# Two groups of vector work moved in the merging stage of a fused decoder block: the sums of a weight pair, and the split of one weight unit behind the third gate

## The chip, the cores and the metric

The kernel runs on one core of a Trainium2 chip. A core has a matrix engine (PE, with its weight loads shown apart as PEld), a vector engine (DVE), a scalar engine (ACT), a small general engine (POOL), and an engine that mostly issues transfers (SP, whose queue is called SPq). They run side by side; each takes its own instructions strictly in the order in which the program lists them, and they wait for each other through semaphores. The metric is the time of one execution in microseconds, as the median of several runs.

## The reference, cut to what matters

The program computes one decoder layer for 256 positions of 1024 features in float32: a SwiGLU feed-forward part, a mixing part with two branches, a second feed-forward part and a final norm. The change lies in the mixing part:

```python
n = rmsnorm(h, mix_norm[l])
z = n @ w_in[l]
q, k, v = z[..., :512], z[..., 512:1024], z[..., 1024:1536]
attn = moba_attention(to_heads(q), to_heads(k), to_heads(v))        # causal, 8 heads
zg = gelu(z[..., 1536:])
gm = chunked_spatial_gating(zg[..., :512], zg[..., 512:], ...)      # u * (W_s layernorm(v) + b)
y_attn = attn @ w_branch_attn[l]
y_gmlp = gm @ w_branch_gmlp[l]
gates = sigmoid(n @ w_gate[l] + b_gate[l])                          # 256 x 2048
merged = gates[..., :1024] * y_attn + gates[..., 1024:] * y_gmlp
h = h + merged @ w_out[l]
```

With 256 positions and blocks of 256 keys, the attention is plain causal attention.

## The kernel before, in words

**Precision.** Every float32 product is made from three matmuls: both operands are split into a high part (a rounded copy, made by ACT) and a low part (the rest, made by DVE as source minus high). The helper `split` at L259 records this pair: ACT's `CAST w<-raw` at L260, then DVE's `TENSOR_TENSOR w<-raw,w` at L262. All weights of the layer pass through it once, so most of ACT's and DVE's work is the splitting of weights.

**Weights.** A weight arrives as a unit of two halves. Each half is one load of 512 KB by SP into a buffer called `raw`, of which there are seven in a ring (L182); its split goes to a buffer `w`, of which there are five in a ring (L167). A load can go into its `raw` buffer only when DVE has made the low part of the half that lay there seven halves earlier. `split_half` (L185) records the split of the next half, after asking for the loads that the ring allows; with `later=True` the ACT part is recorded at once and the DVE part when the caller calls back. `unit(i, ahead)` (L221) records all splits up to unit i + ahead that haven't been recorded yet, so a call of it with nothing left to do records nothing.

**Pairs.** For some weights a scheme with seven products instead of eight is used. It needs sums and differences of the weights: the unit with the word "sums" is made from two loaded halves by four additions on DVE (L209 to L212, 128 x 512 each), and then split like a loaded one (`CAST w<-sum`, `TENSOR_TENSOR w<-sum,w`). For the columns u (of the spatial gating) and v (of the attention), there are two such pairs; the change concerns the sums of the second.

**Order of work.** PE, SP and, in the mixing part, also ACT and DVE take their instructions in the order in which the Python code records them (`in_order`, and the schedule in `kernel`). There is no planner there: to move a line in the code moves its instructions on the engine's queue.

**The mixing part in the order of time.**

- The chunks q, k and gv (the input of the layer norm in the spatial gating) are multiplied. q and k are scaled by ACT and transposed by DVE (`turn_qk`, L845: ACT L848, DVE L849), written to DRAM and read back in another layout (`qback`, and kT inside the tile `qk`; the read back is `from_way`, L566).
- gv goes through a gelu on ACT (L979) and `layer_norm` on DVE (from L951 on). The pair product `accuv` gives u and v (DVE L432 to L446). Then come the scores `sc` of the attention (PE L863; their evacuation is ACT L869 and DVE L870), the spatial mix `mix`, the exponents (ACT L880) and the probabilities with their transposes (DVE L890, L893), which go to DRAM and come back by keys.
- The four gate chunks `g` (512 columns each) are multiplied. For each, `gate` (L926) records first the ACT half of some splits of later weights, if it is asked for them, then two DVE evacuations (L931) and two sigmoids on ACT (L933), then the DVE half of those splits.
- In between, the gating's output is transposed, written to DRAM and read back as `gmback`; `settle_in` (L575) splits it into the tile `gm` (`gmT` in the code).
- `attend` (L937) gives `po`, split into the tile `ao`. `merge` (L1037) multiplies `gm` with the branch weights bg (`pg`) and `ao` with the branch weights ba (`pa`), first for columns 0 to 511, then for 512 to 1023; DVE gates both (L1043, L1054), adds them (L1055) and transposes them (L1056) into `mt`, which goes to DRAM (`mway`) and comes back split as `mg`.
- The output projection follows (`down_features`, `acc`, L229 and L234), in four units of two blocks of `mg` each, and then the second feed-forward part, which takes the rest of the time.

The units after the gates are, in this order, bg0, ba0, bg1, ba1 (two halves each), then four units `out`.

Of the kernel before, what the change touches and what calls it, by code (L numbers as in the profile page):

```python
# [10 lines left out]
F32 = mybir.dt.float32  # L11
# [7 lines left out]
P = 128  # L19
# [34 lines left out]
def block_kernel(ctx, tc, t, out):  # L54
    nc = tc.nc
# [3 lines left out]
    sump = ctx.enter_context(tc.tile_pool(name="sump", bufs=2))  # L59
# [7 lines left out]
    def bank(name):  # L67
        return psum.tile([P, 512], F32, tag="ps", name=name)
# [42 lines left out]
    def add_units(name, n):  # L111
        first = len(units)
        units.extend((name, i) for i in range(n))
        return first
# [25 lines left out]
    muv = len(units)  # L140
    units.extend(("uvs", i, what) for i in range(PAIR_UV) for what in ("single", "sums"))
    units.extend([("u", 0), ("v", 0)])
    mg = add_units("gate", 8)
# [12 lines left out]
    def kind(i):  # L156
        return units[i][2] if len(units[i]) > 2 else None

    parts, raws = {}, {}
# [25 lines left out]
    def split_half(later=False):  # L185

        i, hf = divmod(done_to[0], 2)
        if hf == 0:
            unit_tile(i)
        fetch_to(done_to[0] + RAW)  # L190
        done_to[0] += 1
        if kind(i):
            return quarters(i, hf)
        w, sl = parts[i], half(i, hf)
        return split(w[:, sl, 0, :], w[:, sl, 1, :], raws.pop((i, hf)), later)

    def quarters(i, hf):

        w = parts[i]
        if kind(i) == "single":  # L200
            r = raws[i, hf].rearrange("p one (n c) -> p (one n) c", c=512)
            r, to = (r, w[:, 1:3]) if hf else (r[:, :1], w[:, :1])
        else:
            if hf == 0:
                (a, b), (c, d) = ([r[:, 0, n:n + 512] for n in (0, 512)] for r in [raws.pop((i - 1, k)) for k in range(2)])
                for k in range(2):
                    raws[i, k] = sump.tile([P, 2, 512], F32, tag="sum", name=f"sum{i}_{k}")
                first, second = raws[i, 0], raws[i, 1]
                nc.vector.tensor_add(first[:, 0], a, b)  # L209
                nc.vector.tensor_add(first[:, 1], b, d)  # L210
                nc.vector.tensor_add(second[:, 0], first[:, 0], d)
                nc.vector.tensor_add(second[:, 1], second[:, 0], c)  # L212
            r, to = raws.pop((i, hf)), w[:, 2 * hf:2 * hf + 2]
        return split(to[:, :, 0, :], to[:, :, 1, :], r)

# [5 lines left out]
    def unit(i, ahead=PAIRED):  # L221
        split_to(i + 1 + ahead)
        return parts[i]
# [29 lines left out]
    def mm3(ps, st, mv_, first, last):  # L253
        (sh, sl), (mh, ml) = st, mv_
        nc.tensor.matmul(ps, sh, mh, start=first, stop=False)  # L255
        nc.tensor.matmul(ps, sh, ml, start=False, stop=False)  # L256
        nc.tensor.matmul(ps, sl, mh, start=False, stop=last)  # L257

    def split(hi, lo, src, later=False):  # L259
        nc.scalar.copy(hi, src)  # L260
        def rest():
            nc.vector.tensor_sub(lo, src, hi.bitcast(F32))  # L262
        return rest if later else rest()

    def alloc_T(name, tags):

        return [act.tile([P, 4, 2, S], F32R, tag=tag, name=f"{name}{c}") for c, tag in enumerate(tags)]
# [4 lines left out]
    def block_of(nT, k):  # L272
        return both_of(nT, k)[:, 0, :], both_of(nT, k)[:, 1, :]
# [278 lines left out]
    def chunk(i0, nT, name, c, us=range(2), ps=None, apart=1, ahead=ALONE):  # L552

        if ps is None:
            ps = [bank(f"{name}_{c}{j}") for j in range(NT)]
        for u in us:
            w = unit(i0 + 2 * c + apart * u, ahead)
            for k in range(4):  # L560
                for j in range(NT):
                    st = tuple(p[:, j * P:(j + 1) * P] for p in block_of(nT, 4 * u + k))
                    mm3(ps[j], st, (w[:, k, 0, :], w[:, k, 1, :]), u + k == 0, u == 1 and k == 3)
        return ps
# [7 lines left out]
    def by_token(way):  # L572
        return way.rearrange("(j p) a n -> p j (a n)", p=P)

    def settle_in(to, back):  # L575

        to = to.rearrange("p k two (q c) -> p two q k c", c=32)
        split(to[:, 0], to[:, 1], back.rearrange("p q (k c) -> p q k c", c=32))
# [86 lines left out]
    for k in range(KB):  # L665
# [3 lines left out]
        x, w, g = row[:, :S], row[:, S:], front[:, k:k + 1]  # L669
# [78 lines left out]
    nT2 = alloc_T("n2", ("nA", "nB"))  # L748
# [3 lines left out]
    with in_order():  # L752
# [30 lines left out]
        for n, (at, s) in enumerate(f1d):  # L783
# [6 lines left out]
            else:  # L790
# [3 lines left out]
                for slot, j in [(x, j) for j in range(NT) for x in slots] if ends else [(x, j) for x in slots for j in range(NT)]:  # L794
                    f, b = divmod(slot, len(REST))
# [33 lines left out]
        def tokens(blocks):  # L829
            return blocks.rearrange("p (j a) t -> p j (a t)", j=NT)  # L830
# [14 lines left out]
        def turn_qk(i, ps):  # L845
            by_tokens = tokens(mix_a[:, 8 + 4 * i:12 + 4 * i])
            for j in range(NT):
                nc.scalar.activation(by_tokens[:, j], ps[j], AF.Copy, scale=rs2[j])  # L848
                nc.vector.transpose(qk_turned[i][:, j], by_tokens[:, j])  # L849
# [76 lines left out]
        def gate(g, ps, splits=0):  # L926

            c = slice(g * 512, (g + 1) * 512)
            lows = [split_half(True) for _ in range(2 * splits)]
            for j in reversed(range(NT)):  # L930
                nc.vector.scalar_tensor_tensor(gates[:, j, c], ps[j], rs2[j], gates[:, 0, c],  # L931
                                               op0=ALU.mult, op1=ALU.add)
                nc.scalar.activation(gates[:, j, c], gates[:, j, c], AF.Sigmoid)  # L933
            for low in lows:
                low()
# [29 lines left out]
        turn_qk(0, psq)  # L965
        chunk(mk, nT2, "k", 0, [1], psk, 3, DEEP)
        nc.sync.dma_start(by_token(qk_way[0]), qk_turned[0])
        turn_qk(1, psk)
        nc.sync.dma_start(by_token(qk_way[1]), qk_turned[1])
        q_back = tmp.tile([P, S // 32, P], F32, tag="back", name="qback", bufs=1)  # L970
# [44 lines left out]
        gm_back = tmp.tile([P, S // 32, P], F32, tag="back", name="gmback", bufs=1)  # L1015
        from_way(gm_back, gm_way)
        gate(1, chunk(mg, nT2, "g", 1, [1], psg), 1)
        gate(2, chunk(mg, nT2, "g", 2), 1)
        settle_in(gmT, gm_back)
        gate(3, chunk(mg, nT2, "g", 3))  # L1020

# [221 lines left out]
```

## Time and profile before

| | |
|---|---|
| median of 3 runs | 516.3 us (516.11 to 516.36) |
| profiled execution, its own time | 516.4 us |
| span of its instructions | 514.7 us |
| PE busy | 505.0 us (98%) |
| DVE busy | 462.1 us (90%) |
| ACT busy | 309.9 us (60%) |
| mean granted PE clock | 0.993 |

The profiled execution took 1.7 us more than the span from its first to its last instruction. Times in the profile count from the span's start. "Idle before" in square brackets behind a row is the time in which the engine stood still before that instruction, with what ended it. A row with "x4" merges four instructions in a row; its time is that of the group. Busy times of PE overlap a little, since matmuls are pipelined.

### The profile page before, as it was taken

How to read it: one execution, taken by the hardware profiler on the slowest of the kernel's cores; microseconds unless marked ns; L12 is line 12 of the kernel's file. 1: busy time of each engine (PE TensorE's matmuls, PEld its weight loads, DVE VectorE, ACT ScalarE, POOL GpSimd, SP SyncE). 2: the span in 40 equal slices, each digit the busy share in tenths (PEclk: the TensorE clock that was granted, in tenths of full speed). 3: DMA queues.
4: the chain of work that ended last, by engine and by line, in shares of the span. 5: the costliest groups of instructions: out<-in, count | busy, mean ns of one | idle time of the engine just before them, and what ended most of it. 6: DMA issues, size and time to landing. Idle time of an engine off the chain costs nothing.

```text
span 514.7 us, 6830 instructions
## 1 busy us (share of the span) xinstructions
PE 505.0 (98%) x2314; PEld 418.7 (81%) x2314; DVE 462.1 (90%) x675; ACT 309.9 (60%) x444; POOL 11.2 (2%) x25
## 2 busy tenths in 40 slices
PE   9999999999999999999999999999999999999995
PEld 6888888888888888888888877888888888888884
DVE  6898999999997989799894876998989989999995
ACT  7985549646564766765952803768635756565533
POOL 0010000000000010000000000001000000000001
PEclk9999999999999999999999998999999999999998
DMA  8998588798765987786789765937789648998402
GB/s 317 375 330 327 156 276 258 267 307 280 228 220 179 308 282 291 184 291 245 232 218 304 287 202 171 295 120 260 257 274 300 213 140 274 350 327 251 177 1 82
DMA packets 63987, 126.82 MB, mean 246 GB/s; under 512 B 11729, under 2 KB 36817, under 8 KB 63825
## 3 DMA queue, kind: packets, MB, share of 16 engines
q1 hardware_dynamic: 63664, 126.06, 74.4%
q8 instruction: 18, 0.29, 0.3%
q10 hardware_dynamic: 288, 0.33, 0.2%
q14 instruction: 17, 0.13, 0.1%
HBM read 113.26 MB, written 13.11 MB: 246 GB/s over the span
## 4 chain that ended last, share of the span: by engine, by line
PE 94%; DVE 2%; DMA 2%; issue 1%; ACT 1%; SPq 0%; POOLq 0%; DVEq 0%; POOL 0%; ACTq 0%
PE f L255 12%; PE f L257 12%; PE f L256 12%; PE accdown L257 4%; PE accdown L255 4%; PE accdown L256 4%; PE acch L257 3%; PE acch L255 3%; PE acch L256 3%; PE acc L229 3%; PE g L255 3%; PE g L256 3%; PE g L257 3%; PE acc L234 1%; PE accuv L256 1%; PE accuv L257 1%
## 5 line engine op out<-in xcount | busy, mean ns | idle before, releaser
L262 DVE TENSOR_TENSOR w<-raw,w 128x1024 fp32r<-128x1024 f32 (+1 forms) x180 | 202.7, 1163 | 18.0 <-ACT w L260 17.6
L260 ACT CAST w<-raw 128x1024 fp32r<-128x1024 f32 (+1 forms) x180 | 173.2, 1007 | 31.4 <-DMA raw<-in_ba 8.3
L257 PE MATMUL f<-w,n 128*128 128x512 f32 x272 | 105.8, 389 | 0.0
L255 PE MATMUL f<-w,n 128*128 128x512 f32 x272 | 105.8, 389 | 0.0
L256 PE MATMUL f<-w,n 128*128 128x512 f32 x272 | 105.8, 389 | 0.0
L257 PEld LDWEIGHTS f<-w,n 128*128 128x128 f32 x272 | 51.1, 188 | 10.7
L256 PEld LDWEIGHTS f<-w,n 128*128 128x128 f32 x272 | 51.1, 188 | 10.6
L255 PEld LDWEIGHTS f<-w,n 128*128 128x128 f32 x272 | 51.1, 188 | 10.5
L260 ACT CAST w<-sum 128x1024 fp32r<-128x1024 f32 x34 | 35.8, 1052 | 37.6 <-DVE sum L210 29.5
L262 DVE TENSOR_TENSOR w<-sum,w 128x1024 fp32r<-128x1024 f32 x34 | 41.0, 1216 | 0.5 <-ACT w L260 0.5
L256 PE MATMUL accdown<-w,f1h 128*128 128x512 f32 x68 | 26.5, 389 | 0.0
L257 PE MATMUL accdown<-w,f1h 128*128 128x512 f32 x68 | 26.5, 389 | 0.0
L255 PE MATMUL accdown<-w,f1h 128*128 128x512 f32 x68 | 26.5, 389 | 0.0
L255 PE MATMUL g<-w,n 128*128 128x512 f32 x64 | 25.0, 391 | 0.0
L257 PE MATMUL g<-w,n 128*128 128x512 f32 x64 | 24.9, 389 | 0.0
L256 PE MATMUL g<-w,n 128*128 128x512 f32 x64 | 24.9, 389 | 0.0
L256 PE MATMUL acch<-w,f2h 128*128 128x512 f32 x59 | 23.0, 389 | 0.0
L257 PE MATMUL acch<-w,f2h 128*128 128x512 f32 x59 | 23.0, 389 | 0.0
L255 PE MATMUL acch<-w,f2h 128*128 128x512 f32 x59 | 23.0, 389 | 0.0
L229 PE MATMUL acc<-mg,w 128*128 128x512 f32 x64 | 18.7, 420 | 2.2 <-DVE mg L262 2.2
L596 ACT ACTIVATE f2s<-f,rstd 128x256 f32<-128x256 f32 x18 | 8.2, 474 | 14.0 <-PE f L257 13.9
L229 PEld LDWEIGHTS acc<-mg,w 128*128 128x128 f32 x64 | 12.2, 205 | 4.2 <-DVE mg L262 2.4
(291 smaller groups left out, 917.0 us busy)
## 6 DMA issues: line engine op xcount, KB each, us to landing
raw<-in_f SPq DMA_DIRECT2D x72, 512.0 KB, 6.5
raw<-in_f2d SPq DMA_DIRECT2D x22, 512.0 KB, 6.8
raw<-in_gate SPq DMA_DIRECT2D x16, 512.0 KB, 5.9
raw<-in_f1s SPq DMA_DIRECT2D x14, 512.0 KB, 6.4
raw<-in_f1d SPq DMA_DIRECT2D x14, 512.0 KB, 5.0
raw<-in_out SPq DMA_DIRECT2D x8, 512.0 KB, 5.3
raw<-in_f2s SPq DMA_DIRECT2D x6, 512.0 KB, 6.7
f1way<-f1t SPq DMA_DIRECT2D x11, 256.0 KB, 6.3
```

The lines of the kernel that those rows point to most:

```text
L229: nc.tensor.matmul(ps, st, both.rearrange("p two n -> p (two n)"), start=first, stop=last)
L234: nc.tensor.matmul(ps[:, n:], st, both[:, 0, :], start=False, stop=False)
L255: nc.tensor.matmul(ps, sh, mh, start=first, stop=False)
L256: nc.tensor.matmul(ps, sh, ml, start=False, stop=False)
L257: nc.tensor.matmul(ps, sl, mh, start=False, stop=last)
L260: nc.scalar.copy(hi, src)
L262: nc.vector.tensor_sub(lo, src, hi.bitcast(F32))
L596: nc.scalar.activation(sg, ps[j][:, :CH], AF.Silu, scale=rs[j])
```

## The change

Two places are changed.

**The third gate.** `gate(2, ...)` no longer records splits. Before, it put the ACT half of the split of unit ba0 (two halves) ahead of its own evacuation and sigmoids, and the DVE half behind them; `settle_in(gmT, gm_back)` was recorded after that. Now the third gate's evacuation and sigmoids come first, then the split of the gating's input `gm`, and the split of ba0 is recorded after it, when the fourth gate's chunk asks for its weights.

**The second pair's sums.** The four additions move into a function of their own, `quarter_sums`, which is called right after the second half of the chunk k and the issue of q's write to DRAM, ahead of `turn_qk(1, psk)`. When the split of that unit is recorded later, the sums are found made.

```diff
+    def quarter_sums(i):
+        (a, b), (c, d) = ([r[:, 0, n:n + 512] for n in (0, 512)] for r in [raws.pop((i - 1, k)) for k in range(2)])
+        for k in range(2):
+            raws[i, k] = sump.tile([P, 2, 512], F32, tag="sum", name=f"sum{i}_{k}")
+        first, second = raws[i, 0], raws[i, 1]
+        nc.vector.tensor_add(first[:, 0], a, b)
+        nc.vector.tensor_add(first[:, 1], b, d)
+        nc.vector.tensor_add(second[:, 0], first[:, 0], d)
+        nc.vector.tensor_add(second[:, 1], second[:, 0], c)
+
     def quarters(i, hf):
...
-            if hf == 0:
-                (a, b), (c, d) = ([r[:, 0, n:n + 512] for n in (0, 512)] for r in [raws.pop((i - 1, k)) for k in range(2)])
...
-                nc.vector.tensor_add(first[:, 0], a, b)
-                nc.vector.tensor_add(first[:, 1], b, d)
-                nc.vector.tensor_add(second[:, 0], first[:, 0], d)
-                nc.vector.tensor_add(second[:, 1], second[:, 0], c)
+            if hf == 0 and (i, 0) not in raws:
+                quarter_sums(i)
             r, to = raws.pop((i, hf)), w[:, 2 * hf:2 * hf + 2]
...
         chunk(mk, nT2, "k", 0, [1], psk, 3, DEEP)
         nc.sync.dma_start(by_token(qk_way[0]), qk_turned[0])
+        quarter_sums(muv + 3)
         turn_qk(1, psk)
...
         gate(1, chunk(mg, nT2, "g", 1, [1], psg), 1)
-        gate(2, chunk(mg, nT2, "g", 2), 1)
+        gate(2, chunk(mg, nT2, "g", 2))
         settle_in(gmT, gm_back)
         gate(3, chunk(mg, nT2, "g", 3))
```

No instruction is added or removed on any engine, and the order on PE, SP and POOL stays as it was. ACT's queue differs at one place, DVE's at two.

On ACT, at the third gate, it stood so before; `w_2515` is ba0, `w_2556` is bg1, and `mixed` holds the gates here:

```order
L260 CAST w_2482<-raw_1_2366 128x2x512
L260 CAST w_2515<-raw_0_2377 128x2x512
L260 CAST w_2515<-raw_1_2413 128x2x512
L933 ACTIVATE mixed<-mixed 128x512 x2
L260 CAST gm_1866<-gmback 128x8x4x32
L260 CAST w_2556<-raw_0_2417 128x2x512
L260 CAST w_2556<-raw_1_2445 128x2x512
L933 ACTIVATE mixed<-mixed 128x512 x2
```

and now (ba0 is `w_2523` here; line numbers behind the new function are three or four higher):

```order
L263 CAST w_2482<-raw_1_2366 128x2x512
L936 ACTIVATE mixed<-mixed 128x512 x2
L263 CAST gm_1866<-gmback 128x8x4x32
L263 CAST w_2523<-raw_0_2377 128x2x512
L263 CAST w_2523<-raw_1_2413 128x2x512
L263 CAST w_2556<-raw_0_2417 128x2x512
L263 CAST w_2556<-raw_1_2445 128x2x512
L936 ACTIVATE mixed<-mixed 128x512 x2
```

The two casts of ba0 went behind the two sigmoids and the cast of `gm`. On DVE the same place reads before:

```order
L931 SCALAR_TENSOR_TENSOR mixed<-g_2454,rstd_1769,mixed 128x512
L262 TENSOR_TENSOR w_2515<-raw_0_2377,w_2515 128x2x512
L262 TENSOR_TENSOR w_2515<-raw_1_2413,w_2515 128x2x512
L262 TENSOR_TENSOR gm_1866<-gmback,gm_1866 128x8x4x32
L262 TENSOR_TENSOR w_2556<-raw_0_2417,w_2556 128x2x512
```

and now:

```order
L934 SCALAR_TENSOR_TENSOR mixed<-g_2454,rstd_1769,mixed 128x512
L265 TENSOR_TENSOR gm_1866<-gmback,gm_1866 128x8x4x32
L265 TENSOR_TENSOR w_2523<-raw_0_2377,w_2523 128x2x512
L265 TENSOR_TENSOR w_2523<-raw_1_2413,w_2523 128x2x512
L265 TENSOR_TENSOR w_2556<-raw_0_2417,w_2556 128x2x512
```

The low part of `gm` went ahead of the two of ba0. On DVE at the turning of k (the transposes of `mixed` here are k's) it stood so before:

```order
L262 TENSOR_TENSOR w_1924<-raw_1_1820,w_1924 128x2x512
L849 STREAM_TRANSPOSE mixed<-mixed 128x512 x2
L209 TENSOR_TENSOR sum_0_1974<-raw_0_1780 128x512
L210 TENSOR_TENSOR sum_0_1974<-raw_0_1780,raw_1_1820 128x512
L211 TENSOR_TENSOR sum_1_1975<-sum_0_1974,raw_1_1820 128x512
L212 TENSOR_TENSOR sum_1_1975<-sum_1_1975,raw_1_1820 128x512
L262 TENSOR_TENSOR w_1973<-sum_0_1974,w_1973 128x2x512
```

and now:

```order
L265 TENSOR_TENSOR w_1924<-raw_1_1820,w_1924 128x2x512
L202 TENSOR_TENSOR sum_0_1956<-raw_0_1780 128x512
L203 TENSOR_TENSOR sum_0_1956<-raw_0_1780,raw_1_1820 128x512
L204 TENSOR_TENSOR sum_1_1957<-sum_0_1956,raw_1_1820 128x512
L205 TENSOR_TENSOR sum_1_1957<-sum_1_1957,raw_1_1820 128x512
L852 STREAM_TRANSPOSE mixed<-mixed 128x512 x2
L265 TENSOR_TENSOR w_1979<-sum_0_1956,w_1979 128x2x512
```

The four sums went ahead of k's two transposes; the casts of the sums on ACT stayed behind ACT's scaling of k.

More of the change, by code (lines that the diff above doesn't have):

```diff
@@ L203, in quarters @@
         else:
-            if hf == 0:
-                (a, b), (c, d) = ([r[:, 0, n:n + 512] for n in (0, 512)] for r in [raws.pop((i - 1, k)) for k in range(2)])
[L206 to L209, printed above, removed]
-                nc.vector.tensor_add(first[:, 1], b, d)
-                nc.vector.tensor_add(second[:, 0], first[:, 0], d)
-                nc.vector.tensor_add(second[:, 1], second[:, 0], c)
+            if hf == 0 and (i, 0) not in raws:
+                quarter_sums(i)
             r, to = raws.pop((i, hf)), w[:, 2 * hf:2 * hf + 2]
```

## The prediction

> **What bounds the kernel now.** I read the waits of PE first, then its granted clock around the one wait that counts, then the chain of waits back from there.
>
> ```profile
> PE acc L229 <- DVE mg L262: 2.2, 1, 2.2
> 309.00:310.00 1.00, 0.02 (x1) 0.03 (x1) 0.50 (x2) 0.71 (x2) 0.00 (x0) 0.84 0.57 130
> 310.00:311.00 1.00, 1.00 (x3) 0.81 (x4) 0.86 (x2) 0.00 (x0) 0.00 (x0) 0.50 0.62 175
> 313.00:314.00 1.00, 1.00 (x8) 0.87 (x8) 0.97 (x2) 0.69 (x1) 0.00 (x0) 0.95 0.69 279
> ```
>
> In the waits, the columns are total, times and longest. Past the warm-up PE stands still once: 2.2 us, before the output projection. In the stretches the clock is the third number from the right: 0.84 from 309, 0.50 from 310, 0.95 from 313. The pause thus costs a second time, in matmuls at half speed. Everything else is PE at work, so a gain must come from this place, and a loss from a new pause.
>
> ```profile
> 309.98 3.54 PE L229 MATMUL acc<-mg,w 128*128 128x512 f32 x8 [2.20 <-DVE mg L262]
> 313.35 1.12 PE L234 MATMUL acc<-mg,w 128*128 128x256 f32 x8
> 322.68 3.84 PE L229 MATMUL acc<-mg,w 128*128 128x512 f32 x16
> 326.35 2.08 PE L234 MATMUL acc<-mg,w 128*128 128x256 f32 x16
> 321.42 0.76 DVE L262 TENSOR_TENSOR mg<-mixed,mg 128x256 fp32r<-128x256 f32 x2 [2.34 <-ACT mg L260]
> ```
>
> PE is done with merging at 309.98 - 2.20 = 307.78 and starts the projection at 309.98. Its first eight matmuls take 313.35 - 309.98 = 3.37 us; sixteen later ones take 326.35 - 322.68 = 3.67, so eight at full clock 1.84. The slow clock costs 3.37 - 1.84 = 1.53 us. The last row is the next thing due: the third unit of the projection (PE, 322.68) needs the third piece of `mg`, whose first half is there at 321.42 + 0.76/2 + some 0.05 = 321.85. That leaves 0.8 us of slack.
>
> The chain back from the pause:
>
> ```profile
> 301.54 0.72 DVE mt L1056
> 306.67 2.29 DMA mixed<-mway
> 309.50 0.44 DVE mg L262
> ```
>
> The merged values leave DVE at 302.26 and need 7.2 us through DRAM and the split. Before that, from 288 on, DVE has no long break and waits only for ACT's casts, which themselves follow its evacuations: whatever it has done earlier brings PE's start forward one for one, until the pause is used up.
>
> **The third gate: removed wait, added wait.** ACT first, then DVE, then the landing of `gmback` (last column, from issue):
>
> ```profile
> 273.58 1.05 ACT L260 CAST w<-raw 128x1024 fp32r<-128x1024 f32 x1 [1.36 <-DMA raw<-in_ba]
> 281.56 1.05 ACT L260 CAST w<-raw 128x1024 fp32r<-128x1024 f32 x1 [6.93 <-DMA raw<-in_ba]
> 282.52 1.15 ACT L933 ACTIVATE mixed<-mixed 128x512 f32<-128x512 f32 x2
> 283.57 1.03 ACT L260 CAST gm<-gmback 128x1024 fp32r<-128x1024 f32 x1
> 284.51 2.00 ACT L260 CAST w<-raw 128x1024 fp32r<-128x1024 f32 x2
> 274.84 1.22 DVE L262 TENSOR_TENSOR w<-raw,w 128x1024 fp32r<-128x1024 f32 x1
> 282.65 1.22 DVE L262 TENSOR_TENSOR w<-raw,w 128x1024 fp32r<-128x1024 f32 x1 [6.59 <-ACT w L260]
> 284.63 1.22 DVE L262 TENSOR_TENSOR gm<-gmback,gm 128x1024 fp32r<-128x1024 f32 x1 [0.76 <-ACT gm L260]
> 285.77 2.35 DVE L262 TENSOR_TENSOR w<-raw,w 128x1024 fp32r<-128x1024 f32 x2
> 288.05 1.53 DVE L931 SCALAR_TENSOR_TENSOR mixed<-g,rstd,mixed 128x512 f32<-128x512 f32 x2
> 269.55 2.15 SPq L570 DMA_DIRECT2D gmback<-gmway  x4
> gmback<-gmway SPq DMA_DIRECT2D x2, 128.0 KB, 9.3
> ```
>
> ACT's cast of ba0's second half waits 6.93 us for its load, and holds behind it the sigmoids, whose input is there since 274.9, and the cast of `gm`. DVE idles 6.59 us, then 0.76 more.
>
> Now the sigmoids run at about 274 to 275.5, and ACT waits for `gmback`: the last of its four loads is issued at some 271.2 and lands 9.3 later, at 280.5. Behind that wait now stand both casts of ba0, those of bg1, the fourth gate's sigmoids and the casts of `ao`; behind them DVE. ACT's cast of `gm`: 280.5 to 281.5. DVE: the low part of `gm` from 281.6, 1.14 (285.77 - 284.63), then four halves at 1.14 (288.05 - 285.77, halved), which ACT supplies every 1.0 us: 281.6 + 5 x 1.14 = 287.3 against 288.05. DVE now does one half more behind the wait, but starts a microsecond earlier and without the hole. The term is **0.75 us**. Its bounds: 0.95 - 1.14 = -0.2 if only the sigmoids' place in front of the casts is won and the moved half is paid in full, and 1.4 if `gmback` lands as early as its first load does (269.55 + 9.3 = 278.9), with PE's fourth gate long done. I take 0.75, since landing and durations are those of the same instructions.
>
> What is late now: ba0's first half is freed at 281.6 + 2 x 1.14 = 283.9 instead of 276.06, and seven halves on the `raw` ring stands the second half of the first `out` unit.
>
> ```profile
> raw<-in_out SPq DMA_DIRECT2D x2, 512.0 KB, 9.1
> 291.19 5.81 ACT L260 CAST w<-raw 128x1024 fp32r<-128x1024 f32 x6
> ```
>
> It was issued near 279.8. Issued at 283.9 with the same 9.1 us it lands at 293.0; ACT wants it fourth of its six casts, at 291.19 + 3 x 0.97 = 294.1, less the 0.75: 293.35. That is covered by 0.3 us; without the cover each us late is a us on the chain. ba0 itself is first read by PE after `pg`, near 291, six us after its split.
>
> **The sums ahead of k's turning.**
>
> ```profile
> 208.06 1.39 DVE L849 STREAM_TRANSPOSE mixed<-mixed 128x512 f32<-128x512 f32 x2 [2.02 <-ACT mixed L848]
> 209.37 0.65 DVE L209 TENSOR_TENSOR sum<-raw 128x512 f32<-128x512 f32 x1
> 211.87 2.43 DVE L262 TENSOR_TENSOR w<-sum,w 128x1024 fp32r<-128x1024 f32 x2
> 215.07 0.69 DVE L951 BATCH_NORM_STATS2 st<-mixed 128x6 f32<-128x512 f32 x1 [0.77 <-ACT mixed L979]
> 207.34 1.37 ACT L848 ACTIVATE mixed<-k,rstd 128x512 f32<-128x512 f32 x2 [2.55 <-PE k L257]
> 213.06 1.28 ACT L979 ACT_TABLE_LOAD   x1
> 214.35 1.26 ACT L979 ACTIVATE mixed<-gv,rstd 128x512 f32<-128x512 f32 x2
> 212.35 0.39 PE L257 MATMUL gv<-w,n 128*128 128x512 f32 x1
> ```
>
> The sums take 211.87 - 209.37 = 2.5 us. They fill the 2.02 us hole before 208.06: 206.05 to 208.55, and push k's transposes back by 0.5, and with them SP's write of k, the reads back and the first gate loads, all needed several us later. ACT casts the sums right after k's scaling, from 208.7, instead of at 210.7; the gelu's table is in at 212.0 instead of 214.35, and the gelu starts when PE has gv's first half, 212.74, at some 212.85. The layer norm on DVE starts at 213.5 instead of 215.07: 1.5 us. From there to 237 DVE has only the two short waits inside the layer norm, so 1.5 goes on until the scores:
>
> ```profile
> 237.18 2.60 DVE L870 TENSOR_TENSOR mixed<-sc,mask 128x512 f32<-128x512 f32 x6
> 239.71 2.35 DVE L262 TENSOR_TENSOR w<-raw,w 128x1024 fp32r<-128x1024 f32 x2
> 236.75 1.17 ACT L869 COPY mixed<-sc 128x256 f32<-128x256 f32 x4
> 237.79 2.02 ACT L260 CAST w<-raw 128x1024 fp32r<-128x1024 f32 x2
>   DVE uv L446: 0.5, 2
> 251.53 2.36 DVE L262 TENSOR_TENSOR w<-raw,w 128x1024 fp32r<-128x1024 f32 x2 [1.22 <-ACT w L260]
> ```
>
> PE's scores set the pace here: ACT's copies (L869) end with the last score, now 237.8. The fifth row is what PE's weight loads waited for in the scores, 0.5 us for DVE, and this wait goes too. So ACT's next casts start near 237.4 and end their first at 238.45, and DVE takes it up at 238.5 instead of 239.71: **1.2 us** is left. The softmax, the transposes to keys and the gating's way through DRAM are then bound by DVE and ACT (the 1.22 at 251.53 is ACT's exponents, which move along), and the loads behind them by what DVE frees. Bounds: 0, if the loads up to 281 keep their times, and 1.5. I take 1.2.
>
> **The sum.** The chain comes 0.75 + 1.2 = 1.95 us earlier. The pause shrinks from 2.2 to 0.25 us, or to 0.75 where PE too comes 0.5 earlier out of the scores, which brings nothing as long as it must wait. I take it that so short a pause leaves the clock alone: 1.53 more. PE would be at the third unit at 322.68 - 1.95 - 1.53 = 319.2; the third piece of `mg` is there at 321.85 - 1.95 = 319.9, and PE starts on it at 319.95. So PE's gain there is 1.95 + 0.8 = 2.75 us, and the stages behind run as before. 516.4 of the profiled execution less 2.75 is 513.65; the median is 0.1 below it: **513.6 us**.
>
> **The clock.** A pause of 2.2 us brought the clock to 0.50 for about 3.4 us (from 309.7 to 313.1 by the stretches). [...]
>
> **Rivals.**
>
> 1. *The slow clock stays* (14%). The only row is one pause of 2.2 us; nothing shows where the limit lies. Then PE reaches the third unit at 320.7, after its piece, and the gain is 1.95: 514.35.
> 2. *The sums bring nothing by 288* (16%). For it: loads are saturated around the third gate, and a load that keeps its time holds ACT (6.93). Against it: their issues follow DVE. The gain is 0.75 + 0.8 = 1.55 (514.75, 10%), or 0.75 with the slow clock (515.55, 6%).
> 3. *The late `out` half* (6%). If it takes 10.6 instead of 9.1, 1.2 us late past its cover, the gain is 2.75 - 1.2: 514.75.
> 4. *No change* (14%). The sums bring nothing, and `gmback` lands half a microsecond later, since the loads around it start earlier too: 0.25 is left, 516.0. The waits then only change their names.
> 5. *Slower* (8%). ACT's queue now stands behind `gmback`, and with it bg1, the fourth gate and `ao`, where it stood behind ba0. Each microsecond that this landing comes after 280.5 is one on the chain; at 280.5 + 1.95 = 282.45 the gain is gone. At 284, the pause is 2.2 + 1.55: 517.9. Against it: `gmback` is issued ahead of ba0's half, which landed at 281.5.
>
> **How the numbers follow.** The forecast has 42%, the rivals the rest. 0.2% (1.0 us) is about what this measurement can tell from no change. Faster by more: 42 + 14 + 10 + 6 = 72%; within it: 6 + 14 = 20%; slower: 8%. The range goes from 512.7 (both upper bounds, 1.4 + 1.5 = 2.9, use up the pause, and the third piece of `mg` with its 0.8 decides: 516.4 - 3.7) to 516.0, which takes in all but the slower case.
>
> **What would show it.** The sums right: the layer norm's first row near 213.5, the first DVE split behind the scores near 238.5. The gate right: ACT's cast of `gm` straight at `gmback`'s landing, the two splits of ba0 behind it, the fourth gate's L931 near 286.1. The pause: PE's wait for `mg` between 0.25 and 0.75 us, no stretch with a clock of 0.5, and a new wait of about 0.7 us at the third unit. I'd be wrong if a load holds ACT for longer behind `gmback`, if L931 stays at 288, or if PE waits anew in the feed-forward part, where no wait is seen now.

## The result, and the profile after

The changed kernel takes **512.77 us** (median of 6 runs, 511.86 to 513.65) where the kernel before takes 516.2 (6 runs, 514.57 to 517.01). The ratio is 0.9942 (95% interval 0.9923 to 0.9961): faster by about 3 us. The profiled execution took 513.14 us with a span of 511.4, against 516.4 and 514.7. Line numbers of the changed kernel are three or four higher.

The waits of PE in the profile after (total, times, longest); the last two rows are those of its weight loads between 300 and 325 us:

```profile
PE warm L105 <- DVE zeros L102: 1.2, 1, 1.2
PE f L701 <- ACT n L677: 0.2, 1, 0.2
...
PEld acc L232 <- DVE mg L265: 0.4, 2, 0.2
PEld acc L232 <- DVE mixed L1058: 0.3, 1, 0.3
```

The 2.2 us for `mg` are gone. What is left in this stage are short holds of weight loads, 0.7 us in all.

The stretches of the profile after around the start of the projection; the clock is the third number from the right:

```profile
307.00:308.00 1.00, 0.98 (x7) 0.73 (x6) 0.91 (x3) 0.37 (x2) 0.00 (x0) 1.00 0.65 148
309.00:310.00 1.00, 1.00 (x8) 0.88 (x8) 1.00 (x3) 1.00 (x2) 0.00 (x0) 1.00 0.83 229
```

PE is busy but for 0.02 us and its clock stays at 1.00.

The rows of the projection in the timeline after (start, duration), with the third piece of `mg` that its third unit needs, and the first feed-forward matmul behind it:

```profile
307.57 2.11 PE L232 MATMUL acc<-mg,w 128*128 128x512 f32 x8
309.52 1.12 PE L237 MATMUL acc<-mg,w 128*128 128x256 f32 x8
319.34 3.94 PE L232 MATMUL acc<-mg,w 128*128 128x512 f32 x16
...
318.86 0.76 DVE L265 TENSOR_TENSOR mg<-mixed,mg 128x256 fp32r<-128x256 f32 x2 [2.41 <-ACT mg L263]
...
330.62 0.39 PE L258 MATMUL f<-w,n 128*128 128x512 f32 x1
```

In the timeline before, that last row reads:

```profile
333.85 0.39 PE L255 MATMUL f<-w,n 128*128 128x512 f32 x1
```

PE begins the projection 2.41 us earlier, is another 1.42 ahead after its first eight matmuls (309.52 against 313.35; part of that is given back to the short holds), stands 3.34 ahead at the third unit and 3.23 ahead at the feed-forward part. The spans differ by 3.3. All of the gain is made before 320 us; 0.1 of it is lost up to the feed-forward part, and nothing behind that, which takes 180.8 us in both profiles.

The chain that leads there, after, in order of time: the first row of the layer norm, the first splits behind the scores, the third gate's last sigmoid and what follows it on ACT, the same place on DVE, and the first piece of `mg`. The last row is the landing of `gmback` from its issue:

```profile
213.93 0.69 DVE L954 BATCH_NORM_STATS2 st<-mixed 128x6 f32<-128x512 f32 x1 [1.46 <-ACT mixed L983]
238.72 2.36 DVE L265 TENSOR_TENSOR w<-raw,w 128x1024 fp32r<-128x1024 f32 x2
273.46 0.63 ACT L936 ACTIVATE mixed<-mixed 128x512 f32<-128x512 f32 x1 [0.16 <-DVE mixed L934]
279.21 1.05 ACT L263 CAST gm<-gmback 128x1024 fp32r<-128x1024 f32 x1 [5.12 <-DMA gmback<-gmway]
280.17 3.89 ACT L263 CAST w<-raw 128x1024 fp32r<-128x1024 f32 x4
280.30 1.23 DVE L265 TENSOR_TENSOR gm<-gmback,gm 128x1024 fp32r<-128x1024 f32 x1 [6.87 <-ACT gm L263]
281.44 4.63 DVE L265 TENSOR_TENSOR w<-raw,w 128x1024 fp32r<-128x1024 f32 x4
285.98 1.53 DVE L934 SCALAR_TENSOR_TENSOR mixed<-g,rstd,mixed 128x512 f32<-128x512 f32 x2
289.13 5.81 ACT L263 CAST w<-raw 128x1024 fp32r<-128x1024 f32 x6
307.09 0.76 DVE L265 TENSOR_TENSOR mg<-mixed,mg 128x256 fp32r<-128x256 f32 x2 [4.06 <-ACT mg L263]
...
gmback<-gmway SPq DMA_DIRECT2D x4, 128.0 KB, 8.6
```

The layer norm comes 1.14 us earlier than before, the splits behind the scores 0.99, the fourth gate's evacuation (L934, was 288.05) 2.07, the first piece of `mg` 2.41. These times count from the span's start, and this execution comes to the mixing part 0.42 us later than that of before: its first matmul of gv starts at 191.92 instead of 191.50. Counted from there, the layer norm comes 1.56 us earlier. Over all fourteen profiles gv starts between 191.39 and 192.07, so a difference of up to 0.7 us between two profiles can have its origin ahead of the change. ACT now waits for `gmback` ahead of four casts of weights, as the change says. Its six casts from 289.13 have no wait in them: the late half of `out` is there in time.

### The profile page after: what moved, and what is told of

It reads as the page before. It is cut to its first block, busy times and chain, and to the rows that moved or that the text cites. A ratio compares the mean times of both kernels' runs of the same rounds, so it can differ in the third digit from the quotient of the medians.

```text
span 511.4 us, 6830 instructions
## 1 busy us (share of the span) xinstructions
PE 503.8 (99%) x2314; PEld 417.8 (82%) x2314; DVE 461.3 (90%) x675; ACT 309.5 (61%) x444; POOL 11.2 (2%) x25
## 4 chain that ended last, share of the span: by engine, by line
PE 93%; DVE 3%; DMA 2%; issue 1%; SPq 1%; ACT 0%; POOLq 0%; DVEq 0%; POOL 0%; ACTq 0%
PE f L260 12%; PE f L259 12%; PE f L258 12%; PE accdown L259 4%; PE accdown L258 4%; PE accdown L260 4%; PE acch L260 4%; PE acch L259 4%; PE acch L258 3%; PE g L260 3%; PE g L258 3%; PE g L259 3%; PE acc L232 2%; PE accuv L259 1%; PE accuv L258 1%; PE accuv L260 1%
## 5 line engine op out<-in xcount | busy, mean ns | idle before, releaser
L232 PE MATMUL acc<-mg,w 128*128 128x512 f32 x64 | 17.5, 398 | 0.1
L263 ACT CAST mg<-mixed 128x256 fp32r<-128x256 f32 x8 | 2.8, 402 | 20.2 <-DMA mixed<-mway 20.2
```

What stands on the lines that cost most here:

```text
L232: nc.tensor.matmul(ps, st, both.rearrange("p two n -> p (two n)"), start=first, stop=last)
```

## The experiments

Three sets were run, each on a chip of its own. Two questions: what each part is worth, and how far the gain depends on the granted clock behind the pause. The mean granted clock of an execution tells whether the clock was lost: a loss of 3.4 us at 0.5 is 1.7 us of clock, or 0.003 of the mean. The eleven profiled executions without it have 0.996 to 0.998, the three with it 0.993 and 0.994; the other runs are sorted by this, at 0.995, and at the border a single one can be misread. The rest of the spread costs nothing: in all fourteen profiles the clock also falls 1.7 to 3.9 us before the span's end, when PE has done its last matmul.

| kernel (set) | median us (runs) | lowest to highest | ratio to before, 95% | at 0.995 or less |
|---|---|---|---|---|
| before (1) | 515.12 (35) | 514.24 to 516.81 | | 5 |
| the third gate alone (1) | 514.74 (11) | 514.10 to 515.07 | 0.9986 to 1.0003 | 0 |
| the sums alone (1) | 514.53 (12) | 513.70 to 517.14 | 0.9985 to 1.0011 | 3 |
| changed, chain later by 0.72 (1) | 513.73 (11) | 512.57 to 514.38 | 0.9963 to 0.9983 | 0 |
| changed, chain later by 1.43 (1) | 514.17 (11) | 513.08 to 515.60 | 0.9968 to 0.9990 | 0 |
| before (2) | 515.21 (26) | 514.23 to 517.70 | | 7 |
| before, built once more (2) | 515.49 (12) | 513.62 to 517.85 | 0.9986 to 1.0021 | 5 |
| changed, once more (2) | 513.18 (8) | 512.69 to 514.59 | 0.9951 to 0.9980 | 0 |
| changed, chain later by 2.15 (2) | 514.88 (12) | 512.90 to 517.77 | 0.9980 to 1.0017 | 5 |
| changed, ba0's first half early (2) | 511.99 (5) | 511.77 to 512.13 | 0.9926 to 0.9954 | 0 |
| before (3) | 515.58 (23) | 514.70 to 517.72 | | 5 |
| the third gate alone, again (3) | 514.57 (12) | 512.91 to 516.22 | 0.9955 to 0.9985 | 0 |
| the sums alone, again (3) | 513.93 (12) | 512.66 to 516.27 | 0.9955 to 0.9989 | 2 |
| before, ba0's halves parted (3) | 513.22 (6) | 512.70 to 514.54 | 0.9935 to 0.9970 | 0 |
| changed, a third time (3) | 513.06 (6) | 512.15 to 514.36 | 0.9928 to 0.9969 | 0 |

### The parts alone

The third gate alone:

```diff
-        gate(2, chunk(mg, nT2, "g", 2), 1)
+        gate(2, chunk(mg, nT2, "g", 2))
```

> Only the third gate's split is moved; the sums stay behind k's turning. Theory (each part brings the chain to the projection forward by its own term): in the changed kernel the fourth gate's evacuation came 2.07 us earlier by the clock of the trace, of which 0.99 were there already at the first split behind the scores; so the gate alone is worth about 1.1 us. The pause before the projection shrinks from 2.2 to about 1.1 us, and the score waits of 0.5 stay. If a pause of 1.1 us spares the clock, PE is at the third unit after its piece is due no later than now: gain 1.1 + 0.8 = 1.9 us against the kernel before. Rival A (a shorter pause costs the clock as well): granted clock 0.5 behind the pause, gain 1.1 us. Rival B (the gate's move is what brought nearly all): pause below 0.3 us and gain about 3 us.

> The gate's part alone once more, now beside the changed kernel on one chip. The turns on the chain gave 0.55, 0.99 and about 1.4 us for 0.72, 1.43 and 2.15 us. Theory (one chain): this kernel's chain is the sums' 1.2 us behind that of the changed kernel, so it is 0.8 us above the changed kernel. Rival (the parts need each other; the first measurement, 0.4 us below the kernel before in the median, was no accident): 1.4 us or more above it.

The sums alone (the changed kernel with the third gate as before):

```diff
+        quarter_sums(muv + 3)
         turn_qk(1, psk)
...
         gate(2, chunk(mg, nT2, "g", 2), 1)
```

> Only the sums of the second pair are moved ahead of k's turning; the third gate keeps its two splits. Theory: the layer norm starts 1.1 to 1.5 us earlier, the first split behind the scores about 1.0 to 1.4 earlier, and everything behind follows, the loads around the third gate too, so that ba0's second half lands about 1 us earlier. Pause 2.2 - 1.2 + up to 0.6 that PE itself comes earlier out of the scores: 1.0 to 1.6 us. Gain 1.2 + 0.8 = 2.0 us with the clock spared. Rival A (the clock falls at such a pause too): gain about 1.2 us. Rival B (the loads keep their times, the sums bring nothing by the third gate): the pause stays at 2.2 or more, gain 0.

> The sums' part alone once more, beside the changed kernel. Theory (one chain): 1.1 us behind on the chain, so 0.75 us above the changed kernel in executions that keep the clock, and one execution in five or so loses it (mean clock 0.995 or less) and takes 1.5 us more. Rival (the parts need each other): 1.4 us or more above the changed kernel also where the clock is kept.

The timeline of the gate alone (first execution): the low part of `gm` and the fourth gate's evacuation on DVE, and the projection's first and third unit on PE:

```profile
281.26 1.23 DVE L262 TENSOR_TENSOR gm<-gmback,gm 128x1024 fp32r<-128x1024 f32 x1 [6.51 <-ACT gm L260]
286.95 1.53 DVE L931 SCALAR_TENSOR_TENSOR mixed<-g,rstd,mixed 128x512 f32<-128x512 f32 x2
308.39 2.12 PE L229 MATMUL acc<-mg,w 128*128 128x512 f32 x8 [0.50 <-DVE mg L262]
320.33 3.92 PE L229 MATMUL acc<-mg,w 128*128 128x512 f32 x16
```

And of the sums alone (first execution):

```profile
287.00 1.53 DVE L934 SCALAR_TENSOR_TENSOR mixed<-g,rstd,mixed 128x512 f32<-128x512 f32 x2
308.24 2.12 PE L232 MATMUL acc<-mg,w 128*128 128x512 f32 x8 [1.09 <-DVE mg L265]
320.04 3.92 PE L232 MATMUL acc<-mg,w 128*128 128x512 f32 x16
```

At the fourth gate's evacuation the gate alone brings 288.05 - 286.95 = 1.10 us, the sums alone 1.05, both together 2.07: the two terms add up. In the second executions the rows are at 286.97 and 286.74. Each part leaves a pause, and its median lies between that of before and that of the changed kernel. How far between is not settled: in set 1 neither part can be told from no change (medians 0.4 and 0.6 below before, where 1.9 and 2.0 were expected), in set 3 both can (1.0 and 1.6 below). Both expectations counted 0.8 us that come of the lost clock in the profile of before, which most runs don't pay; that is a part of the miss and not all of it. Against the 513.1 of the changed kernel (median of its 20 runs in three series) the gate alone stands 1.5 to 1.6 higher, the sums alone 0.8 to 1.4; set 1 has no run of the changed kernel on its chip, and the medians of before differ by up to 0.5 between the chips. In set 3, beside the changed kernel, the gate alone is 1.5 above it, where one chain gave 0.8 and the rival 1.4 or more: by the median it is the rival's figure. The sums alone are 0.9 above it, and 0.5 in the ten runs that kept the clock. Why the gate alone gains so little in the median, when its two profiles show 1.1 us on the chain, stays open. The executions of these rows took 514.10 and 513.82 us, 1.0 and 0.7 above the profiled one of the changed kernel, which is just what their third units come later; the medians scatter around that.

### The same program with and without its clock

The two executions of the sums alone show what sets the pause apart from DVE's work. SP's queue in the first (issue of the four writes of `mt`, then of the reads back):

```profile
299.18 2.84 SPq L1062 DMA_DIRECT2D mway<-mt  x4
303.52 3.77 SPq L573 DMA_DIRECT2D mixed<-mway  x8
```

And in the second, with the projection's first matmuls behind it:

```profile
298.93 2.85 SPq L1062 DMA_DIRECT2D mway<-mt  x4
304.62 3.78 SPq L573 DMA_DIRECT2D mixed<-mway  x8
...
309.14 3.10 PE L232 MATMUL acc<-mg,w 128*128 128x512 f32 x8 [1.83 <-DVE mg L265]
313.60 1.08 PE L232 MATMUL acc<-mg,w 128*128 128x512 f32 x4
```

The reads start 0.08 us after the third of the four writes has landed, which completes the first of two pieces. From the end of the writes' issues to the reads it is 303.52 - 302.02 = 1.50 us in the first and 2.84 in the second, in the same program with the writes issued a quarter of a microsecond earlier. By the landings, the difference lies in the load issued just ahead of the writes, a half of a feed-forward weight. Its issue, and its time to landing, in the first:

```profile
297.11 0.33 SPq L183 DMA_DIRECT2D raw<-in_f  x1
...
raw<-in_f SPq DMA_DIRECT2D x1, 512.0 KB, 5.4
```

And in the second:

```profile
296.85 0.33 SPq L183 DMA_DIRECT2D raw<-in_f  x1
...
raw<-in_f SPq DMA_DIRECT2D x1, 512.0 KB, 6.7
```

The load lands at 302.47 and at 303.57, the first write at 302.80 and at 303.91, and the other three follow at 0.3 us each. In all fourteen profiles the first write lands 0.32 to 0.38 us after this load, which takes 5.4 to 6.7 us. PE stands still for 1.83 us instead of 1.09, and now its clock falls to 0.50: the sixteen matmuls up to 313.60 take 4.46 us, where they take 2.90 in the changed kernel (307.57 to 310.47). The first execution took 513.82 us, the second 515.64.

The kernel before does the same. It was built again, beside the changed one:

> The kernel before, unchanged, traced and timed once more beside the others. In the timing of the parts, 5 of 35 executions of it had a mean granted clock of 0.995 or less and took 516.3 us or more; the other 30 lay between 514.2 and 516.0 at 0.996 to 0.999. Theory (the half clock behind the pause comes in some executions only): with a mean clock of 0.996 or more the trace shows the pause of about 2.2 us with the clock at 1.0 behind it, PE waits 0.5 to 0.8 us at the third unit of the projection, and the span is about 513.1. Rival (the executions differ by the length of the pause): pause of 1.5 us or less in a fast execution.

> The changed kernel, unchanged, on the same chip as the kernel before and the two kernels below. Theory (chain 2.0 to 2.4 us earlier, no pause left): 1.9 to 2.4 us below the kernel before where that keeps its clock, so about 513 against 515, and no execution with a mean clock of 0.995 or less. Rival (each part alone gave 0.3 us or less in the median, so both give little here too): 0.6 us or less.

> The changed kernel once more, as the reference for the three above. Expected: 0.9966 of the kernel before, with the interval 0.995 to 0.998 that the last comparison gave; no execution with a mean clock of 0.995 or less.

The rows of before, built once more, in its profiled execution (mean clock 0.998):

```profile
310.23 2.14 PE L229 MATMUL acc<-mg,w 128*128 128x512 f32 x8 [1.41 <-DVE mg L262]
322.18 2.12 PE L229 MATMUL acc<-mg,w 128*128 128x512 f32 x8
```

And those of the changed one in the same set:

```profile
307.70 2.11 PE L232 MATMUL acc<-mg,w 128*128 128x512 f32 x8 [0.59 <-DVE mg L265]
319.47 3.94 PE L232 MATMUL acc<-mg,w 128*128 128x512 f32 x16
```

Here the pause before the change is 1.41 us, and the first eight matmuls run at full clock (2.14 instead of 3.54). The expectation had this pause at 2.2 us in an execution that keeps its clock; the rival had it at 1.5 or less, and that is what came. It is shorter mainly because PE leaves merging at 308.82 instead of 307.78: 0.57 of that is there at gv already, and most of the rest comes from its wait for `gm` in `pg`. So the profile on which the prediction rests is of one kind of execution, and not of the more frequent one. Of 96 runs of before in the three sets, 22 have a mean clock of 0.995 or less; these take 516.26 us or more, while the medians of the rest are 514.7 to 515.1. The clock is not all that makes a run late: the profiled execution above kept it and took 515.99 us, and in set 3 four runs with 0.996 to 0.999 took 516.04 to 517.08. None of the changed kernel's 20 runs has 0.995 or less.

### A longer chain, to find the limit

The changed kernel, with DVE's last transpose ahead of `mway` made two, three or four times over into the same place, 0.72 us each; the values are the same. Below the form with one repeat, with 3 and 4 in place of 2 in the other two:

```diff
-                    nc.vector.transpose(m_turned[:, j, c:c + n], m)
+                    for _ in range(2 if hf == 0 and j else 1):
+                        nc.vector.transpose(m_turned[:, j, c:c + n], m)
```

> The changed kernel with the last transpose of the first merging half made twice (same values written again), which puts 0.72 us of DVE work on the chain to the projection. Theory: the pause of PE, 0.02 us in the changed kernel, becomes about 0.7 us, the clock stays at 1.0, and since the third piece of the merged values comes 0.72 later too, the time grows by about 0.7 us against the changed kernel. Rival A (a pause of 0.7 us is enough to lose the clock): a granted clock of 0.5 behind the pause, time 0.7 + 1.5 less the 0.7 that PE now waits at the projection's later units: about 1.5 us more. Rival B (the chain does not bound PE any more): no pause, time as in the changed kernel.

> The same with that transpose made three times: 1.43 us on the chain. Theory: pause about 1.4 us; with the clock spared the time is 1.4 us above that of the changed kernel. Rival A (the clock falls): about 1.4 + 1.5 - 0.7 = 2.2 us above it. Rival B (the chain does not bound): same time as the changed kernel.

> The changed kernel with the last transpose of the first merging half made four times: 2.15 us on the chain. Theory: the pause is back at about 2 us, the time about 2 us above the changed kernel, and some executions (one in seven or more) lose the clock, with a mean of 0.995 or less and some 0.7 us more. Rival (the clock depends on more than the pause's length): none of them loses it.

The medians rise by 0.6, 1.1 and 1.8 us over 513.1, for 0.72, 1.43 and 2.15 us of added work; the first two are compared across chips. The chain is the bound, though by the medians a delay here costs a little less than its length. One place where it is given back can be seen: the last two writes of `mt` land behind a weight load, 2.2 to 3.6 us after their issue; with the repeats, issued later, they land 1.7 to 1.8 us after it. With 2.15 us the changed kernel is as slow as before, and loses its clock as often (5 of 12). Its profiled execution:

```profile
309.54 3.07 PE L232 MATMUL acc<-mg,w 128*128 128x512 f32 x8 [1.92 <-DVE mg L265]
```

The one with 0.72 us, in the waits of PE. Here DVE waited 1.35 us, up to 227.46, for an ACT cast that a load of gate weights held, and its first split behind the scores stands at 239.64, as late as before the change (239.71):

```profile
PE acc L232 <- DVE mg L265: 1.5, 1, 1.5
```

That pause (1.48 us in its row) leaves the clock at 1.00, the one of 1.92 doesn't. Over all fourteen profiled executions the pauses before the projection are 2.20, 1.92 and 1.83 where the clock was lost, and 1.48, 1.41, 1.12, 1.09 and less where it was kept. Whether the length of the pause alone decides is not shown.

### Filling the hole that is left

DVE still stands idle for 6.87 us at 280.30, waiting for `gmback`. The first half of ba0 is loaded long before; only its second half was late. So its split can go between the sigmoids and `gm`:

```diff
         gate(2, chunk(mg, nT2, "g", 2))
+        split_half()
         settle_in(gmT, gm_back)
```

> The changed kernel with one more move: the first half of ba0 is split behind the third gate's sigmoids and ahead of the gating's input, in the time in which ACT and DVE wait for that input. Theory: DVE makes this half's low part in its idle stretch of 6.9 us, the chain comes 1.1 us earlier, the waits of about 0.7 us in all that PE still has at the projection's units go: 0.5 to 0.7 us below the changed kernel. Rival (the pause is used up and nothing else follows the chain): same time within 0.3 us.

And the third gate's change with the same line in the kernel before, without the change to the sums:

> The kernel before with only the third gate changed, and that in the other way: ba0's first half is split behind the sigmoids and ahead of the gating's input, its second half behind it; the sums stay behind k's turning. Theory (one chain, to which each move adds its own term): the gate's 1.1 us and another 1.1 for the half that now fills DVE's idle stretch, 2.2 together, as much as the changed kernel's two parts have; the score waits of PE of 0.5 us stay. So about the time of the changed kernel, 2.0 us below the kernel before. Rival (the sums are needed, since their 1.2 us at the scores reach the loads around the gate): 1 us above the changed kernel or more.

The timeline of the changed kernel with the half early:

```profile
279.81 1.22 DVE L265 TENSOR_TENSOR gm<-gmback,gm 128x1024 fp32r<-128x1024 f32 x1 [3.55 <-ACT gm L263]
280.95 3.77 DVE L265 TENSOR_TENSOR w<-raw,w 128x1024 fp32r<-128x1024 f32 x3
284.64 1.53 DVE L934 SCALAR_TENSOR_TENSOR mixed<-g,rstd,mixed 128x512 f32<-128x512 f32 x2
306.94 2.00 PE L232 MATMUL acc<-mg,w 128*128 128x512 f32 x8
318.10 3.83 PE L232 MATMUL acc<-mg,w 128*128 128x512 f32 x16
```

Three halves stand behind `gm` instead of four; the evacuation comes 1.34 us earlier than in the changed kernel (0.86 of it from the half, 4.63 - 3.77, and 0.49 because the cast of `gm` comes earlier; but 0.44 of it was there at gv, which starts at 191.48 here). PE has no wait at all in this stage, and the third unit comes 1.24 us earlier. The time is **511.99 us**, 1.2 below the changed kernel in the same set, with intervals of the ratio that meet only at the edge (0.9926 to 0.9954 against 0.9951 to 0.9980). That is more than the 0.5 to 0.7 that were expected, and all five runs are faster than each of the changed kernel's eight. It is the best version found. Its five runs lie within 0.36 us, where those of the other kernels spread by one to over four. That would fit a PE that no longer waits, so that the scatter of the transfers doesn't reach the end; five runs don't show it.

In the kernel before, without the sums:

```profile
285.93 1.53 DVE L931 SCALAR_TENSOR_TENSOR mixed<-g,rstd,mixed 128x512 f32<-128x512 f32 x2
319.29 3.90 PE L229 MATMUL acc<-mg,w 128*128 128x512 f32 x16
```

These two rows lie within 0.05 us of those of the changed kernel, and the times by 0.16, 513.22 and 513.06. As far as six runs each can tell, a microsecond on this chain is worth the same, whether it is won at 209 us or at 280.

## Why the prediction was right, and where not

The forecast of 513.6 us stands 0.8 above the median, and the range holds it. Its steps in order:

- **Sums.** 1.5 us at the layer norm, 1.2 at the scores. Counted from the first matmul of gv, the layer norm comes 1.49 to 1.57 us earlier in all nine profiles with the sums moved. (The gelu's table would be in at 212.34, not at 212.0 as the prediction has it, from 213.06 - 2.0 + 1.28; that is still ahead of gv's 212.74.) At the scores it is 1.41 or 1.42 in six of the nine, and 1.02, 0.77 and nothing in the others, where DVE stood still for 0.39, 0.71 and 1.35 us for ACT's casts of gate weights, which waited for their loads. The prediction had no wait there. By 288 the sums alone are worth 1.05 to 1.31. So the step holds, and rival 2 (nothing left by 288) falls for the kernel as a whole; the profile with 0.72 us more shows that it can come true in a single execution.
- **Third gate.** 0.75 us, measured 1.10 and 1.08 alone. The low part of `gm` starts at 281.26 in that run, not at 281.6, and the five parts behind it take what was reckoned (5.69 us to 286.95, against 5 x 1.14). So `gmback` landed some 0.3 earlier than it was put. Its last load took 7.7 to 9.7 us from issue to landing over the fourteen profiles, so a difference of this size is scatter.
- **Pause.** 0.25 to 0.75 us; 0.02, 0.59 and 0 in the three profiles of the changed kernel. In the first, the chain gains 0.34 more behind the evacuation (2.41 at `mg` against 2.07), of which 0.27 is the write to DRAM: from the end of its issues to the reads, 2.23 us before and 1.96 now. The 7.2 us through DRAM that the prediction took for the way of `mt` itself hold the time up to the landing of the weight load ahead of it (the first write landed 0.32 to 0.38 us behind that load in every profile). The sum comes out all the same, since that load is issued 2.07 us ahead of the first write in every profile and so moves with the chain.
- **Next due.** The third unit at 319.95, with a new hold of 0.7 on its piece of `mg`; it is at 319.34, with holds of 0.7 in all, spread over two units. The third piece comes 2.56 us earlier instead of 1.95, and that 0.61 is all by which 2.75 was short of 3.34.
- **Rivals 3, 4 and 5.** The half of `out` is in time: issued at 282.69, it lands in 5.1 us, not in the 9.1 that the prediction took. `gmback` lands earlier, 8.6 us after its issue instead of 9.2, so nothing is lost behind it.
- **Clock.** That so short a pause leaves it alone is right (rival 1 falls): 0 of 20.

**The step that was mis-sized is the 1.53 us of the clock.** It was counted as if each execution of before paid it. It has the right size where it is paid (sixteen matmuls 4.33 to 4.46 us instead of 2.90), but in the three sets only some 23 in 100 runs paid it, the profiled one among them. In the others PE gets to the third unit earlier and waits there for its piece of `mg` (in before, built once more, it starts at 322.18, and the low part of that piece only at 321.70); the chain alone then sets the gain, 1.95 by the prediction's own terms, without the 0.8 us of slack. From 514.93, the median of the runs with their clock in set 2, that gives 512.98 (measured 513.18); from 515.14 in set 3 it gives 513.19 (measured 513.06). In the first comparison, where four of six runs of before took over 516 us (only the clock of the profiled execution is on record, 0.993), the whole 2.75 and a little more was to be seen. So it was luck that the forecast came near the mark: most runs of before in the series that it was set against were about as late as the profile on which it stood. In the two longer sets the gain is 2.0 and 2.5 us in the medians.

## What to carry to other kernels

Where an engine takes its instructions in order, look for work that stands behind a wait for a load though its own input is long there, and for an idle stretch of the next engine behind it; what is ready goes ahead, and what is not goes behind, by halves if need be. Before a cost of a profiled execution goes into a sum, ask whether each execution pays it: the spread of the runs' times and their mean granted clock tell that, and one profile doesn't. Where a pause of PE decides, look for what scatters in front of it; here it is a small write (128 KB) that lands 0.32 to 0.38 us behind a large load (512 KB) issued 2.07 us before it. Whether issuing the write first would help was not tried.

## What the runs showed of the hardware

The slow clock lasted the same time in each of the three profiles in which it came in the middle. The stretches of 0.2 us at its beginning and end, in the profile before:

```profile
309.60:309.80 0.20, 0.00 (x0) 0.00 (x0) 0.20 (x1) 0.17 (x1) 0.00 (x0) 0.70 0.35 73
313.00:313.20 0.20, 0.20 (x2) 0.11 (x2) 0.20 (x1) 0.20 (x1) 0.00 (x0) 0.77 0.89 348
```

In the changed kernel with 2.15 us more on the chain:

```profile
310.40:310.60 0.20, 0.20 (x2) 0.20 (x1) 0.02 (x1) 0.20 (x2) 0.00 (x0) 0.53 1.14 287
313.80:314.00 0.20, 0.20 (x4) 0.20 (x4) 0.20 (x1) 0.00 (x0) 0.00 (x0) 0.94 0.00 0
```

And in the second execution of the sums alone:

```profile
310.00:310.20 0.20, 0.20 (x2) 0.20 (x1) 0.02 (x1) 0.20 (x1) 0.00 (x0) 0.50 0.75 205
313.40:313.60 0.20, 0.20 (x3) 0.20 (x3) 0.17 (x2) 0.00 (x0) 0.00 (x0) 0.97 0.10 41
```

A stretch of 0.2 us with a mean clock of 0.70 has been slow for 0.12 of it, so the first slow time goes from 309.68 to 313.09; the others go from 310.41 to 313.82 and from 310.00 to 313.41. That is 3.41 us each. It does not start with the pause's end: once 0.3 us before it, twice 0.9 behind it, with PE at full work. The 3.41 us ahead of each hold 1.90, 1.92 and 1.83 us of pause; no kept execution has a pause over 1.48.

The clock's record in the traces of the two kernels of the comparison shows one thing more. In the profile before, it begins with a first rise at 5.89 us, and the loss comes 303.79 us later; the slow time lasts 3.413 us by this record, and from its end to the fall at 511.07, behind PE's last matmul, it is 197.97 us. In the profile after, the only fall, at 508.43, comes 501.76 us behind the first rise at 6.67. These three distances are 89.0, 58.0 and 147.0 times the 3.413 us. What sets them is not shown.

If the length of the pause decides, its limit lies between 1.48 and 1.83 us; three losses and eleven executions without one are all that stands behind that.

The other thing not expected is how much one small transfer through DRAM varies between executions: from the end of its issues to the reads, the write of `mt` took 1.50 to 2.84 us in the eleven profiled executions with the transposes as they were, and 0.99 to 1.00 in the three where the last transpose came later by itself. That scatter stands right before the pause and makes it longer or shorter: 1.09 and 1.83 us in the two executions of the sums alone. By the landings it comes from the weight load issued ahead of the write, which lands 5.4 to 6.7 us after its issue; the write lands 0.32 to 0.38 us behind it in every profile. What makes that load take longer in one execution than in another stays open.
